# Order and placement around four TensorE waits in a hybrid conformer and stick-breaking decoder layer

## The chip, the cores and the metric

The kernel runs on one core of a Trainium2 chip. The metric is the device time of one execution in microseconds. The engines are TensorE (PE, with its weight loads shown as PEld), VectorE (DVE), ScalarE (ACT), GpSimd (POOL) and SyncE (SP); SP, ACT and POOL also issue DMAs, each in the order of its own queue. An engine executes its instructions in its program's order, so an instruction that waits holds up all that are queued behind it.

## What is computed

One decoder layer on x of 1024 tokens by 1024 channels, in float32:

```python
sh1, sc1, ga1, sh2, sc2, ga2 = split(silu(c) @ ada_w + ada_b, 6)
h = rmsnorm(x, pre_mix_g) * (1.0 + sc1) + sh1
# hybrid_mixer(h)
glu_in, qkv, gates = split(h @ w_in, ...)           # 1024, 1536 and 2048 columns
u = u_val * sigmoid(u_gate); u = causal_depthwise_conv(u, 31 taps)
y_conv = silu(layernorm(u)) @ w_conv_out
y_att = stick_breaking_attention(q, k, v) @ w_att_out   # 8 heads of 64
merged = sigmoid(g_conv) * y_conv + sigmoid(g_att) * y_att
x = x + ga1 * rmsnorm(merged @ w_o, post_mix_g)
h = rmsnorm(x, pre_ffn_g) * (1.0 + sc2) + sh2
y = (silu(h @ gate) * (h @ up)) @ w_ffn_out          # 2816 hidden channels
x = x + ga2 * rmsnorm(y, post_ffn_g)
```

## The kernel before, in words

Activations lie transposed: channels on the 128 partitions in tiles (index k or n, 8 of them), tokens along the free dimension in two halves of 512. Each float32 operand of a large product is split into a rounded high part (`hi`, a copy on ACT, called a cast here) and a low part (`lo`, the difference, on DVE). A product is then three matmuls, hi·hi, hi·lo and lo·hi, for each 128 rows of depth, so a product of depth 512 and 512 tokens is 12 matmuls. The gate and FFN products use a seven-product block scheme (the names s1 to s4, T1 to T4, B11 to B22, ka, kc): sums of weight blocks (s...) times sums of activation blocks (T..., B...).

Most instructions are put in order by a planner that simulates the engines; it takes what is ready, in the order of the program and of priorities. Some stretches are written out by hand and kept: `pin` ties each instruction of an engine to the one before it. Tiles come from pools; a tile of a tag takes the buffer of the one that had it `bufs` tiles earlier, and waits for that one's last reader. Pools are stacked in SBUF, so a pool that is opened after another was closed lies on the other's memory, and each of its tiles waits for the old tiles that it overlaps.

The stages that the change touches:

1. *Start (0 to 60 us).* PE, ACT and DVE are pinned. Per channel tile k, `shift_pe(k)` computes the shift column with 8 products of an `ada_w` tile (16 records in the trace, line 284), `shift_act(k)` (L288) moves it to `mod`, `x_op`, `hi_op` (L303) and `lo_op` (L306) make hhi[k] and hlo[k], and `gemm_q` (L321) adds the products of tile k to the first q, k and gate banks. Tiles 5 to 7 take their shift from DVE. In the loop over k, `shift_pe(kn + 2)` with kn = k + 1 stands ahead of the products of step k, so at k = 0 it is `shift_pe(3)`.
2. *Early gate products (about 400 to 462 us).* `early(i, q)` runs 14 times, in the order (0,0), (1,0), (0,1), (2,0), (1,1), (3,0), (2,1) and so on. One call casts half of a gate weight (`w_op`, hi on ACT L145, lo on DVE L413), runs a product into bank `k_i` (L426; q = 1 adds to the bank of q = 0), copies the bank to a tile `ee` (ACT, L665) and stores it from ACT's queue (L666). There are three banks, two buffers for `ee` (tag `sg`), three each for weights (`whi`, `wlo`) and raw weights. The planner orders it together with the making of the operands T1 to T4 (L701, L715 to L718).
3. *Hand-ordered FFN start (about 738 to 830 us).* The calls `ke` (early FFN products, L1146), `wh`/`wlo` (cast and low part of a weight, L145/L1079), `e` (copy and store of a result), `t12`, `t3`, `t4` (activation sums, L1165 to L1177), `hi_of`/`lo_of` (L1157/L1161), `b22h`/`b22l` (L1124/L1127) and the steps of two generators `r0 = ffn(0)`, `r1 = ffn(1)` are listed one after the other and pinned on PE, ACT and DVE. `next(r)` runs a generator to its next `yield`; the first step of `ffn(f)` for f > 0 makes the weight sums s1 and s2 on DVE (L1422, L1423) and the cast and low part of s2. Products are at L1037, the adds that take a product at L1439, L1454, L1457 and L1463.
4. *FFN's second product (from about 1160 us).* The pools of the FFN close (pv: eight `y2` tiles of 4 KB per partition, then nine `wt` tiles of 2 KB), and px and pg open in their place. `prep1` makes the operands of the first sweep: weights `wa` (cast L145, low part L1573) and gated activations `gb` (cast L145, low part L1567) in five buffers with the tag `gt`. `sweep` multiplies them at L1581. In px lie the output tiles of the first block (tag `xr`), in pg the operands and the small tiles `acc` and `rs` of the last norm.

Of the kernel before, what the change touches and what calls it, by code (L numbers as in the profile page):

```python
# [10 lines left out]
F32 = mybir.dt.float32  # L11
F32R = mybir.dt.float32r
AF = mybir.ActivationFunctionType
# [4 lines left out]
P = 128  # L18
D = 1024
T = 1024  # L20
KT = D // P
# [48 lines left out]
def tile_block(ctx: ExitStack, tc: tile.TileContext, xT, vecs, ada1, ada2, win, wv, wcv, wat, wo, w1, w2, cvw, out):  # L70
# [126 lines left out]
    with ExitStack() as s0:  # L197
# [119 lines left out]
        def gemm_q(b_, w, k, *sms, cs=(0, 1)):  # L317
            cols = slice(k * P, (k + 1) * P)
            for st, mv in sms:
                for c in cs:  # L320
                    pe.matmul(b_[c], w[st][:, cols], h[mv][k][:, hs[c]], start=(k == 0 and st == 0 and mv == 0),  # L321
                              stop=(k == KT - 1 and mv == 1))
# [31 lines left out]
        for k in range(KT):  # L354
            kn = k + 1
            if kn < KT:
                if kn not in SH_DVE:
                    shift_act(kn)
                if kn + 2 < KT and kn + 2 not in SH_DVE:
                    shift_pe(kn + 2)  # L360
                x_op(kn)
                if kn <= 2:
                    w0_hi(kn)
                hi_op(kn)
                if kn + 1 < KT:
                    dots(kn + 1)
                if kn <= 2:
                    w0_lo(kn)
            if k:
                lo_op(k)  # L370
            store(xm_d[k], xs[k])
            ws = list(zip((q0b, k0b, gg0b), w0s))
            if k == 0:
                gemm_q(*ws[0], 0, LH, HL)
                gemm_q(*ws[1], 0, HH, HL)
            elif k == 1:
                gemm_q(*ws[0], 1, HH, LH)
                gemm_q(*ws[1], 0, LH)
                gemm_q(*ws[1], 1, HH, LH)
                gemm_q(*ws[2], 0, HH, HL)  # L380
                gemm_q(*ws[2], 1, HH)
            else:
                for i, bw in enumerate(ws):
                    if k == 2 and i == 2:
                        gemm_q(*bw, 0, LH)
                        gemm_q(*bw, 1, LH)
                    gemm_q(*bw, k, HH, LH)
                    if k == KT - 1:
                        gemm_q(*bw, k - 1, HL)
                        gemm_q(*bw, k, HL)  # L390
                if k < KT - 1:
                    for bw in ws:
                        gemm_q(*bw, k - 1, HL)
# [16 lines left out]
    def w_op(name, src, hi_eng, lo_eng):  # L410
        t = wp.tile([P, 2, CH], F32R, tag=("whi", "wlo")[next(uid) % 2], name=name)
        copy_to(hi_eng, t[:, 0], src)
        lo_eng.tensor_tensor(t[:, 1], src, t[:, 0], op=ALU.subtract)  # L413
        return t[:, 0], t[:, 1]
# [14 lines left out]
    with ExitStack() as sC:  # L429
        pc = mkpool(sC, "pc")  # L430
        with ExitStack() as sA:
# [215 lines left out]
            for n in PLAIN:  # L647
                gb = banks2(f"pg{n}")
                gemm(gb, load_w(win[20 + n], f"wg{n}"), h, range(KT))
                for c in range(NCH):  # L650
                    sg = sgp.tile([P, CH], F32, tag="sg", name=f"sg{n}_{c}", bufs=2)
                    act.activation(sg, gb[c], AF.Sigmoid, bias=0.0, scale=1.0)
                    act.dma_start(s_d[n][:, c * CH:(c + 1) * CH], sg)
            kes = {}

            def early(i, q):
                if q == 0:
                    raw = wp.tile([P, T], F32, tag="wraw", name=f"ew{i}")
                    load(raw, win[20 + 2 * i])
                    kes[i] = bank(f"k_{i}"), raw  # L660
                k, raw = kes[i]
                w = w_op(f"a1{q + 1}_{i}", raw[:, q * CH:(q + 1) * CH], act, dve)
                prod0(k, w, ("B11", "B21")[q], q == 0)
                e = sgp.tile([P, CH], F32, tag="sg", name=f"ee{q}_{i}", bufs=2)
                act.activation(e, k, (AF.Copy, AF.Sigmoid)[q])  # L665
                act.dma_start(s_d[2 * i][:, :CH] if q else e_d0[i], e)  # L666

            for n, i in enumerate(GPAIRS):
# [258 lines left out]
    with ExitStack() as sF:  # L927
# [144 lines left out]
        def wh(key):  # L1072
            hi = wp.tile([P, T], F32R, tag="whi", name=f"w_{key}_hi")
            copy_to(act, hi, raws[key])
            wes[key] = hi
# [325 lines left out]
        def ffn(f):  # L1401
# [18 lines left out]
            if f:  # L1420
                s1, s2, s3 = wtmp(f"s1_{f}"), wtmp(f"s2_{f}"), wtmp(f"s3_{f}")
                dve.tensor_tensor(s1, a21, a22, op=ALU.add)  # L1422
                dve.tensor_tensor(s2, s1, a11, op=ALU.subtract)  # L1423
            s2o = w_op(f"s2o_{f}", s2, act, dve)
            yield
            s1o = w_op(f"s1o_{f}", s1, act, dve)
# [50 lines left out]
            yield  # L1477

        r0, r1 = ffn(0), ffn(1)
        for j in range(2):  # L1480
            t4(j)
        for j in (0, 1):
            hi_of("T1", j, h2[j, 0])
        ke(6, 1)
        wh(9)
        e(6, 1)
        for j in (2, 3):
            hi_of("T1", j, h2[j, 0])
        for j in range(2):
# [26 lines left out]
            b22h(j)  # L1516
        raw_w(1)
        next(r1)
        next(r0)
        next(r0)  # L1520
        for j in range(HK):
            b22l(j)
        next(r0)
        for j in (2, 3):
            t4(j)
        for j in (2, 3):
            lo_of("T4", j, h2[HK + j, 0])
        next(r1)
# [17 lines left out]
    with ExitStack() as sG:  # L1546
# [8 lines left out]
            return hp.tile([P, 2, CH], dt, tag="act", name=name)  # L1555

        def x_tile(name):
            return px.tile([P, 2, CH], F32, tag="xr", name=name, bufs=4)

        def bank(name):  # L1560
            return psg.tile([P, CH], F32, tag="main", name=name)
# [130 lines left out]
            return po_.tile([P, CH], F32, tag="wt", name=name, bufs=3)  # L1692

        def sum_sq(name, ys):
            acc = pg.tile([P, CH], F32, tag="acc", name=name, bufs=2)
            for n, y in enumerate(ys):
                if n == 0:
                    act.activation(acc, y, AF.Square)
                else:
                    sq = sq_tile(f"{name}_{n}")  # L1700
                    act.activation(sq, y, AF.Square)
                    add(dve, acc, acc, sq)
            return acc

        def finish(c, h, ps_sum, yy, last=None):
            n = ps_sum.shape[-1]
            cols = slice(h * n, (h + 1) * n)
            dcols = slice(c * CH + h * n, c * CH + (h + 1) * n)
            rs = pg.tile([P, CH], F32, tag="rs", name=f"frs{c}{h}", bufs=2)[:, :n]
            m, a = (sq_tile(f"frs{c}{h}{i}")[:, :n] for i in "ma")  # L1710
            rstd_from(rs, m, a, ps_sum, D)
            for m in range(4):
                y = ytile[yy[m // 2], m % 2]
                for i in range(2):
                    yi = y[:, i, cols]
                    if c == 0 and m < 2:
                        dve.tensor_tensor(yi, yi, rs, op=ALU.mult)
                    else:
                        src = last[2 * (m - 2) + i][:, cols] if last else yi
                        dve.scalar_tensor_tensor(yi, src, gpost2[:, 2 * m + i:2 * m + i + 1], rs, op0=ALU.mult,  # L1720
                                                 op1=ALU.mult)
                    if last:
                        add(dve, yi, yi, xq[2 * m + i])
                dst = out[2 * m:2 * m + 2, :, dcols].rearrange("n p t -> p n t")
                if last:
                    load(dst, y[:, :, cols])
                else:
                    acc = nc.gpsimd.dma_start(dst, y[:, :, cols], accum_op=ALU.add)
                    for i in range(2):
                        after_store(acc, c, 2 * m + i)  # L1730
# [142 lines left out]
```

## Time and profile before

| | us |
|---|---|
| median of 3 runs (1391.90 to 1392.66) | 1392.32 |
| the profiled execution | 1392.84 |
| its span, first to last instruction | 1391.1 |
| PE busy in it | 1364.4 |
| DVE busy | 1046.8 |
| ACT busy | 651.6 |
| POOL busy | 107.1 |
| granted clock of PE, mean | 0.997 |

In the profile's rows of the timeline the columns are: start in us from the span's start, duration in us, engine, line of the kernel, operation, tile written <- tiles read with buffer numbers left out, shapes, number of merged instructions (xcount), and in brackets how long the engine stood idle before it and what ended that. The letter q behind an engine marks its queue of DMA issues. Ends of matmuls are modelled, and consecutive ones overlap in the rows: a matmul of 512 columns is listed with 0.39 us while the next one starts 0.227 us after it. A wait is counted only where the engine had nothing left to run. In the rows of a tile, the three numbers before a stretch of time are the shortest, median and longest duration in ns.

### The profile page before, as it was taken

The page shows a single profiled execution, that of the slowest core. Times are in us where ns is not written, and L with a number is a line of the kernel's source. Part 1 is how long each engine was busy: PE and PEld are TensorE (multiplying, and loading weights), DVE is VectorE, ACT ScalarE, POOL GpSimd, SP SyncE. Part 2 cuts the span into 40 slices and gives each one's busy share as a digit, 9 for nine tenths or more (in the row PEclk, how much of TensorE's full clock was granted, in tenths as well). Part 3 has the DMA queues.
Part 4 walks back from the last instruction along what each step waited for, and adds up shares of the span by engine and source line. Part 5 has one row for each costly group of instructions (what it writes and reads, how often), then busy time and mean ns, then how long its engine had stood idle before and what let it go on. Part 6 is the DMA issues. An engine that isn't in the chain of part 4 may idle for free.

```text
span 1391.1 us, 18714 instructions
## 1 busy us (share of the span) xinstructions
PE 1364.4 (98%) x6778; PEld 1146.5 (82%) x6778; DVE 1046.8 (75%) x1600; ACT 651.6 (47%) x1147; POOL 107.1 (8%) x247
## 2 busy tenths in 40 slices
PE   7999999999999999999999999999999999999996
PEld 4898888998987888888887778888888887888886
DVE  7998686775858799777597987778877866784355
ACT  6475565464546457213365543324444444334441
POOL 0100000000000011000012100001111110000002
PEclk9999999999999999999999999999999999999998
DMA  9512051140468546955646545457776779586736
GB/s 384 216 35 80 16 167 46 46 136 32 136 199 304 201 131 239 334 184 194 265 137 195 198 139 179 144 189 253 241 244 245 263 255 389 167 343 218 247 108 122
DMA packets 94940, 265.01 MB, mean 191 GB/s; under 512 B 10048, under 2 KB 21440, under 8 KB 93824
## 3 DMA queue, kind: packets, MB, share of 16 engines
q1 hardware_dynamic: 74352, 201.68, 42.7%
q0 software_dynamic: 17904, 57.42, 11.8%
q10 hardware_dynamic: 2592, 4.72, 0.9%
q8 instruction: 53, 0.87, 0.3%
q14 instruction: 39, 0.32, 0.1%
HBM read 192.74 MB, written 71.04 MB: 190 GB/s over the span
## 4 chain that ended last, share of the span: by engine, by line
PE 93%; DMA 2%; ACT 2%; DVE 2%; issue 1%; SPq 0%; DVEq 0%; ACTq 0%
PE ka L1037 15%; PE ka L1581 9%; PE kc L1037 8%; PE pwo L955 6%; PE pb L1581 4%; PE ke L1146 4%; PE ka L426 4%; PE pgv L166 3%; PE pya L166 3%; PE pyc L777 3%; PE pv L503 3%; PE kc L426 2%; PE k L426 2%; PE pgg L166 2%; PE pk L166 2%; PE pcv L482 2%
## 5 line engine op out<-in xcount | busy, mean ns | idle before, releaser
L577 ACT ACTIVATE ka<-z 128x128 f32<-128x128 f32 (+2 forms) x96 | 47.3, 494 | 44.4 <-PE z L576 33.8
L1581 PE MATMUL ka<-gt,w2f 128*128 128x512 f32 x264 | 63.4, 389 | 0.0
L583 DVE TENSOR_TENSOR_SCAN ka<-ka,eye 128x128 f32<-128x128 f32 (+1 forms) x64 | 51.4, 815 | 11.9 <-ACT ka L577 11.8
L588 DVE TENSOR_TENSOR be<-be,ka 128x127 f32<-128x127 f32 (+2 forms) x96 | 53.8, 573 | 7.1 <-ACT be L579 2.0
L1581 PEld LDWEIGHTS ka<-gt,w2f 128*128 128x128 f32 x264 | 49.6, 188 | 10.3
L121 DVE SCALAR_TENSOR_TENSOR ada<-ada,cb 128x1024 f32<-128x1024 f32 x32 | 38.9, 1222 | 18.0 <-DMA ada<-in_ada_dram 17.8
L579 ACT ACTIVATE be<-z 128x127 f32<-128x127 f32 (+2 forms) x96 | 47.0, 496 | 5.6 <-PE tr L601 5.5
L601 PE MATMUL tr<-ident,be 128*128 128x128 f32 x288 | 46.5, 272 | 0.4 <-DVE be L588 0.4
L1146 PE MATMUL ke<-b,w_hi 128*128 128x512 f32 x176 | 44.5, 395 | 1.1 <-ACT w_hi L145 1.1
L586 DVE TENSOR_TENSOR_SCAN ka<-ka 128x512 f32<-128x512 f32 x32 | 40.6, 1275 | 3.7 <-ACT ka L577 3.6
L482 PE MATMUL pcv<-ph,cvw 128*128 128x128 f32 x320 | 42.9, 275 | 0.0
L607 ACT ACTIVATE ahi<-tr 128x512 fp32r<-128x512 f32 x48 | 28.3, 601 | 27.5 <-PE tr L601 19.4
L482 PEld LDWEIGHTS pcv<-ph,cvw 128*128 128x128 f32 x320 | 40.4, 191 | 0.7
L1146 PEld LDWEIGHTS ke<-b,w_hi 128*128 128x128 f32 x176 | 33.0, 188 | 9.2 <-ACT w_hi L145 1.5
L145 ACT ACTIVATE gt<-X 128x512 fp32r<-128x512 f32 x33 | 20.3, 629 | 39.0 <-DVE X L1624 13.1
L608 DVE TENSOR_TENSOR alo<-tr,ahi 128x512 fp32r<-128x512 f32 x48 | 32.1, 685 | 7.9 <-ACT ahi L607 7.6
L601 PEld LDWEIGHTS tr<-ident,be 128*128 128x128 f32 x288 | 34.8, 140 | 3.8 <-PE z L576 0.7
L145 ACT ACTIVATE s1o<-s 128x512 fp32r<-128x512 f32 x22 | 13.8, 629 | 50.4 <-PE ka L1037 43.5
L503 PE MATMUL pv<-wv_hi,hhi 128*128 128x256 f32 x128 | 36.8, 288 | 0.2 <-DVE klo L543 0.2
L426 PE MATMUL k<-hhi,a 128*128 128x512 f32 x112 | 35.4, 391 | 1.7 <-ACT ee L665 1.6
L503 PE MATMUL pv<-wv_hi,hlo 128*128 128x256 f32 x128 | 36.5, 285 | 0.0
L503 PE MATMUL pv<-wv_lo,hhi 128*128 128x256 f32 x128 | 36.2, 284 | 0.0
(551 smaller groups left out, 4154.9 us busy)
## 6 DMA issues: line engine op xcount, KB each, us to landing
w_d<-w2o POOLq DMA_DIRECT2D x44, 512.0 KB, 7.6
w2f<-w_d SPq DMA_DIRECT2D x44, 512.0 KB, 4.5
ada<-in_ada_dram SPq DMA_DIRECT2D x32, 512.0 KB, 5.5
w2r<-in_w_dram SPq DMA_DIRECT2D x44, 256.0 KB, 3.8
w1g<-in_w_dram SPq DMA_DIRECT2D x21, 512.0 KB, 3.7
w1u<-in_w_dram SPq DMA_DIRECT2D x21, 512.0 KB, 5.4
cvw<-in_cvw_dram SPq DMA_DIRECT2D x20, 512.0 KB, 3.7
ada_w<-in_ada_dram SPq DMA_DIRECT2D x8, 1024.0 KB, 13.8
```

What stands on the lines that cost most here:

```text
L166: pe.matmul(bank, st[:, cols], mv[k][:, c * CH:(c + 1) * CH], start=(i == 0 and s == 0), stop=(i == n - 1 and s == 2))
L426: pe.matmul(bank_, w[st][:, cols], mvs[mv], start=(first and j == 0 and s == 0), stop=(j == HK - 1 and s == 2), skip_group_check=not first)
L482: pe.matmul(cv[:, gi * TM:(gi + 1) * TM], wts[n][:, at:at + P], ph[:, g, SH - 1 - d:SH - 1 - d + TM], start=(d == 0), stop=(d == SH - 1))
L503: pe.matmul(pv[:, :256], st[k][:, tcols], mv[:, wc], start=(k == 0 and i == 0), stop=(k == KT - 1 and i == 2))
L577: act.activation(kap[:, s_lo:s_hi], z[:, zo:zo + w], AF.Sigmoid, bias=0.0, scale=-0.125)
L583: dve.tensor_tensor_scan(rev, rev, eye[:, CH - w:][:, ::-1], 0.0, op0=ALU.mult, op1=ALU.add)
L588: dve.tensor_tensor(beta[:, :m], beta[:, :m], kap[:, s_lo + 1:s_lo + 1 + m], op=ALU.mult)
L601: pe.transpose(tr[:, o:o + P], probs[ii][:, jo:jo + P], ident)
L955: pe.matmul(bank_, st[:, cols], mv[k][:, cs], start=(k == 0 and q == 0), stop=(k == KT - 1 and q == 2))
L1037: pe.matmul(bank_, st[:, cols], t[:, mv], start=(first and j == 0 and s == 0), stop=(j == HK - 1 and s == 2), skip_group_check=not first)
L1146: pe.matmul(kbs[f], wes[f][st][:, cols], t[:, mv], start=(i == 0 and j == 0 and st == 0 and mv == 0), stop=(j == HK - 1 and st == 1), skip ...
L1581: pe.matmul(dst, w[st][:, cols], g[mv], start=first and s == 0, stop=last and s == 2, skip_group_check=more)
```

## The change

Four edits in one:

1. `shift_pe(3)` moves from ahead of the products of k = 0 to behind them. The later ones keep their places.
2. From the fourth call of `early` on, the cast of a call on ACT is placed behind the result copy `ee` of the call three before. It is a tie of order on one engine, not a semaphore.
3. In the hand-written FFN start, `ke(6, 1)`, `wh(9)`, `e(6, 1)` go ahead of the first T4 and T1 operands; `ffn(1)` gets a `yield` between its sums s1, s2 and the cast of s2; the four `b22l` come directly behind those sums, ahead of the first two product steps of r0; the cast of s2 follows `t4(2)`, `t4(3)`.
4. `x_tile` has seven buffers and not four, `acc` and `rs` move from pg to px, and `rs` has three buffers and not two. px grows by 12 KB per partition for `xr` and by 10 KB for the other two, so the `gt` tiles of pg start that much further up.

```diff
@@ start
-                if kn + 2 < KT and kn + 2 not in SH_DVE:
+                if k and kn + 2 < KT and kn + 2 not in SH_DVE:
                     shift_pe(kn + 2)
...
                 gemm_q(*ws[1], 0, HH, HL)
+                shift_pe(3)
@@ early
-            kes = {}
+            kes, ees = {}, []
...
+                begin = len(nc.cur_bb.bb.instructions)
                 w = w_op(f"a1{q + 1}_{i}", raw[:, q * CH:(q + 1) * CH], act, dve)
+                if len(ees) > 2:
+                    for ins in nc.cur_bb.bb.instructions[begin:]:
+                        if ins.engine == mybir.EngineType.Activation:
+                            tc.add_manual_dep(ins, ees[-3], mybir.DependencyInfo(
+                                mybir.DependencyClass.NoSync, mybir.DependencyReason.SCHED_ONLY))
...
-                act.activation(e, k, (AF.Copy, AF.Sigmoid)[q])
+                ees.append(act.activation(e, k, (AF.Copy, AF.Sigmoid)[q]).ins.name)
@@ ffn
                 dve.tensor_tensor(s2, s1, a11, op=ALU.subtract)
+            if f == 1:
+                yield
             s2o = w_op(f"s2o_{f}", s2, act, dve)
...
         r0, r1 = ffn(0), ffn(1)
+        ke(6, 1)
+        wh(9)
+        e(6, 1)
         for j in range(2):
             t4(j)
         for j in (0, 1):
             hi_of("T1", j, h2[j, 0])
-        ke(6, 1)
-        wh(9)
-        e(6, 1)
...
         next(r1)
-        next(r0)
-        next(r0)
         for j in range(HK):
             b22l(j)
         next(r0)
+        next(r0)
+        next(r0)
         for j in (2, 3):
             t4(j)
+        next(r1)
         for j in (2, 3):
             lo_of("T4", j, h2[HK + j, 0])
@@ second product
-            return px.tile([P, 2, CH], F32, tag="xr", name=name, bufs=4)
+            return px.tile([P, 2, CH], F32, tag="xr", name=name, bufs=7)
...
-            acc = pg.tile([P, CH], F32, tag="acc", name=name, bufs=2)
+            acc = px.tile([P, CH], F32, tag="acc", name=name, bufs=2)
...
-            rs = pg.tile([P, CH], F32, tag="rs", name=f"frs{c}{h}", bufs=2)[:, :n]
+            rs = px.tile([P, CH], F32, tag="rs", name=f"frs{c}{h}", bufs=3)[:, :n]
```

## The prediction

> **What bounds the kernel now.** I read the page's engine list and its chain first, then the waits of TensorE (PE), then the order of time around each wait.
>
> ```profile
> span 1391.1 us, 18714 instructions
> PE 1364.4 (98%) x6778; PEld 1146.5 (82%) x6778; DVE 1046.8 (75%) x1600; ACT 651.6 (47%) x1147; POOL 107.1 (8%) x247
> ...
> PE 93%; DMA 2%; ACT 2%; DVE 2%; issue 1%; SPq 0%; DVEq 0%; ACTq 0%
> ```
>
> PE is busy 1364.4 of 1391.1 us and makes up 93% of the chain that ended last. The change takes no matmul away, so it can win only from the 26.7 us in which PE stands still, plus small stretches hidden inside "busy". The waits of PE over the whole span:
>
> ```profile
> PE psh L284 <- DMA ada_w<-in_ada_dram: 2.8, 2, 1.6
> ...
> PE k L426 <- ACT ee L665: 1.6, 1, 1.6
> PE ka L1581 <- ACT gb L145: 1.2, 1, 1.2
> PE ke L1146 <- ACT w_hi L145: 1.1, 1, 1.1
> PE ka L1037 <- DVE uw L1454: 0.5, 1, 0.5
> ```
>
> Columns: who waited, for whom, us in total, how often, the longest. These five rows hold 7.2 us, and each part of the change lies on one or two of them. Nothing later than these is tied to an absolute time: behind a mended wait, loads follow buffers that PE itself frees. So I count a gap closed on PE as time won at the end, unless the next operand is late there.
>
> One unit is used throughout, a product of 12 matmuls of 512 columns:
>
> ```profile
> 821.72 2.72 PE ka L1037 x12
> ```
>
> That is 2.72 us, 0.227 a matmul, when PE runs without gaps.
>
> **Part 1: the fourth shift product goes behind the k = 0 products.** It removes nothing; 16 matmul records (2.0 us) change place in PE's order, and no DMA and no other engine's instruction moves.
>
> ```profile
> 28.55 2.02 PE L284 MATMUL psh<-csb,ada_w 128*128 128x128 f32 x16 [1.58 <-DMA ada_w<-in_ada_dram]
> ...
> 32.26 1.95 PE L284 MATMUL psh<-csb,ada_w 128*128 128x128 f32 x16
> ...
> 58.99 0.62 PE L321 MATMUL pq<-hhi,w0hi 128*128 128x512 f32 x2
> ...
> 26.91 1.28 DVE L306 SCALAR_TENSOR_TENSOR hlo<-x,mod,hhi 128x1024 fp32r<-128x1024 f32 x1
> ...
> 57.13 2.59 DVE L306 SCALAR_TENSOR_TENSOR hlo<-x,mod,hhi 128x1024 fp32r<-128x1024 f32 x2
> ...
> 57.25 1.15 ACT L303 ACTIVATE hhi<-x,mod 128x1024 fp32r<-128x1024 f32 x1 [3.97 <-DVE x L300]
> ```
>
> PE now stands 1.58 us for the ada tile at 28.55, runs that product, then eight matmuls of k = 0 (1.8 us), then the next shift product at 32.26. After the change the eight come first. They need the low part of h, which VectorE (DVE) delivers at 26.91 + 1.28 = 28.19. So they run from 28.2 to 29.6 (the first two a little before), the shift product from 29.6 to 31.4, and PE is 1.0 us ahead at the second one. That lead is not kept whole. DVE has no idle time in this stretch and sets the rate: the high part for k = 7 is there at 57.25 + 1.15 = 58.40, where PE now arrives at about 59.1, and the last low part at 57.13 + 2.59 = 59.72. PE can gain 0.7 at the first and about 0.55 at the second, where what was the shift wait becomes a wait for hhi. Ends: 0 (DVE takes all of it) and 1.0. I take **-0.55**, nearest to the row of the last low part. The shift column of k = 3 is read two steps later on ScalarE (ACT), so its delay of 1 us is covered there; without that cover it would cost the same 1 us again.
>
> **Part 2: early gate casts after the result copy three calls back.** It adds order alone; ACT's 14 casts and 14 copies stay.
>
> ```profile
> 421.10 0.33 ACTq L653 DMA_DIRECT2D s_d<-sg  x1
> ...
> 425.18 0.58 ACT L665 ACTIVATE ee<-k 128x512 f32<-128x512 f32 x1
> 426.03 0.60 ACT L665 ACTIVATE ee<-k 128x512 f32<-128x512 f32 x1 [0.27 <-DMA s_d<-sg]
> ...
> 433.35 0.57 ACT L665 ACTIVATE ee<-k 128x512 f32<-128x512 f32 x1
> ...
> 418.61 0.39 PE L426 MATMUL k<-hhi,a 128*128 128x512 f32 x1
> ...
> 433.97 0.50 PE L426 MATMUL k<-hhi,a 128*128 128x512 f32 x1 [1.61 <-ACT ee L665]
> ```
>
> ```profile
> L145 ACT ACTIVATE a<-ew x14: 615/626/634, 397.9 to 443.4; 128x512 fp32r<-128x512 f32 x14
> L413 DVE TENSOR_TENSOR a<-ew,a x14: 680/684/693, 398.5 to 444.1; 128x512 fp32r<-128x512 f32 x14
> ...
> DMA to landing us min/median/max: 2.0/4.1/6.7
> ```
>
> (The last row is of the copies' stores: from issue to landing.) PE's sixth early product waits 1.61 us for the third copy, which stood on ACT behind casts for later products. With the tie those casts come behind it. But two things speak against booking 1.61. First, a copy also needs one of two buffers, freed when a store lands: the second copy visibly waited for a landing, and the first copy's store, issued no earlier than 425.8, may land as late as 432.5, so the third copy may hardly come earlier than that. Second, today the third product that PE runs, at 418.61 + 2 x 2.72 = 424.05, is the one of call 3 (its bank is free and its cast was made long before; the casts begin at 397.9). Its cast is now tied behind the first copy, which came at 425.18. PE then has only call 2 left, which adds to the bank that this copy reads: a new wait from 424.05 to 425.2 or 425.75, 1.1 to 1.7 us. Afterwards the loop is copy 0.6 + cast 0.63 + low part 0.68 + product 2.72 = 4.6 us against three products, 8.2 us, so 3.5 us are left for a late landing. Behind each tied cast on ACT stand later casts and copies, and on SP the loads of the next gate weights move by up to 7 us, since their buffers are freed by the casts; by my estimate the first weight pair of the next stage then still lands some 3 us before its product. Ends: -1.6 (wait gone, none new) and +1.7 (new one, old one kept). I take **-0.2**: one wait given for another.
>
> The row gives 4.1 us for a store of 256 KB. [...]
>
> **Part 3: the hand-ordered FFN start.** No instruction is added; the order on ACT and DVE (pinned here) changes, PE's order does not. SP's and POOL's DMAs only follow their buffers, earlier.
>
> ```profile
> 784.04 0.64 ACT L1157 ACTIVATE T_0o<-y 128x512 fp32r<-128x512 f32 x1 [1.47 <-DVE y L1177]
> ...
> 786.28 1.04 ACT L145 ACTIVATE w_hi<-w_raw 128x1024 fp32r<-128x1024 f32 x1
> ...
> 787.37 2.11 PE L1146 MATMUL ke<-b,w_hi 128*128 128x512 f32 x8 [1.07 <-ACT w_hi L145]
> ...
> 787.35 1.22 DVE L1079 TENSOR_TENSOR w_lo<-w_raw,w_hi 128x1024 fp32r<-128x1024 f32 x1 [1.29 <-ACT w_hi L145]
> ```
>
> Moving ke(6,1), wh(9), e(6,1) ahead puts the cast of weight 9 before the four T4/T1 casts. Its buffer is weight 6's, last read by ke(6,1), the last product but one before the wait (786.14 - 5.44 = 780.7 to 783.4, where 786.14 is the wait's start less the modelled tail of 0.16); ACT idled 1.47 us until 784.04, so the cast fits at 782.6 to 783.6 and the T casts hardly move. The low part then ends near 787.2; PE, starting at 786.14, wants it eight matmuls in, at 787.95. The wait goes: -1.07, next late is nothing.
>
> ```profile
> 801.11 0.84 PE L1037 MATMUL ka<-T_0o,s2o 128*128 128x512 f32 x3
> ...
> 814.31 1.24 PE L1037 MATMUL ka<-T_2o,a 128*128 128x512 f32 x3
> ...
> 816.09 0.85 PE L1037 MATMUL ka<-T_0o,s2o 128*128 128x512 f32 x3
> ...
> 804.96 0.69 DVE L1028 TENSOR_TENSOR s2o<-s,s2o 128x512 fp32r<-128x512 f32 x1 [2.59 <-ACT s2o L145]
> ...
> 810.75 0.75 DVE L1127 SCALAR_TENSOR_TENSOR B_3o<-y,mod,B_3o 128x512 fp32r<-128x512 f32 x1
> ...
> 812.01 0.69 DVE L1454 TENSOR_TENSOR uw<-ka,uw 128x512 f32<-128x512 f32 x1
> ...
> 814.72 0.69 DVE L1161 TENSOR_TENSOR T_3o<-y,T_3o 128x512 fp32r<-128x512 f32 x1
> ```
>
> The five products of f = 0 run from 801.11 to 816.09, 14.98 us against 5 x 2.72 = 13.60: 1.38 lost at the end, on B22's low parts, on uw and on T4's low parts. The cause is DVE: it idles 2.59 us for the cast of f = 1's s2, then does everything late. In the new order the four B22 low parts (2.65 us) fill that hole. With PE 1.07 ahead, T3 ends at 808.2 and uw's add runs at 808.4 to 809.1, now bound by PE; then two T4 operands on DVE (1.4), two casts and the s2 cast of f = 1 on ACT (0.6 each), the s2 low part, and T4's low parts end at 812.95 and 813.55. B22 runs to 810.92 without a wait, and T4's third operand is wanted at 812.5: 0.45 still lost. Gain 1.38 - 0.45 = 0.93. If the s2 low part is slower to come, T4's lows wait behind it and the gain falls to 0.3; the ends of the part are -1.07 and -2.45. I take **-2.0**. f = 1's own products want s2's low part at 814.1, 1.8 us after it is there.
>
> **Part 4: where the gated operands' tiles lie.** No operation moves in the program; the pool px grows by three x tiles and takes acc and rs, so the tiles "gt" of pg start higher: over the FFN's short-lived weight temporaries instead of over its y2 tiles, which hold p1, uw and the w2 forms until their stores land.
>
> ```profile
> 1161.76 0.63 ACT L145 ACTIVATE wa<-wa 128x512 fp32r<-128x512 f32 x1 [1.36 <-PE ka L1037]
> 1162.29 2.70 ACT L145 ACTIVATE gb<-X 128x512 fp32r<-128x512 f32 x5
> ...
> 1162.96 1.20 PE L1581 MATMUL ka<-gb,wa 128*128 128x512 f32 x4 [1.24 <-ACT gb L145]
> ...
> 1148.77 0.68 DVE L1028 TENSOR_TENSOR s4o<-s,s4o 128x512 fp32r<-128x512 f32 x1
> ```
>
> All five first gb casts stand behind a weight cast that waits for the FFN's last product. The temporaries' last read is at 1148.77, so the planner can put the casts before 1161 on an ACT that idles between its jobs. Then PE starts at once: 1.24, plus about 0.3 inside the first four matmuls (1.20 against 0.91), where the low part is late. The next limit may be the bank that the FFN's last add on DVE still reads then. Ends: 0 (order unchanged) and -1.5; I take **-1.3**, near the wait's row. rs with three buffers and acc's place change nothing: PE runs into the tail without waiting for them.
>
> **Sum.** -0.55 - 0.2 - 2.0 - 1.3 = -4.05. The profiled execution took 1392.84 (span 1391.1 and 1.74 around it), 0.52 above the median 1392.32. Against its own time the sum is 1388.8; against the median **1388.3**.
>
> **Rivals.** (a) *Absorbed or reordered*: the planner makes the unpinned orders anew from parts 2 and 4, and PE, which lost almost nothing there, meets a new wait of about the size of those in the table (1 to 1.6), or part 4's casts stay behind the weight cast. Then only parts 1 and 3 minus one wait remain: 1392.3 - 2.55 + 1.2 = 1391.0, within 0.2%. For it: the table holds only four waits behind part 1, so a new order has little to win. Against: the orders in parts 1 and 3 are written out, not planned. (b) *Buffers, not order*: the early stage's wait lies on two store buffers, so the tie only moves it; part 2 gives +1.5 (new wait kept, old one nearly kept) while the rest holds: 1390.0, the same side as (a). [...]
>
> ```profile
> 461.41 0.60 ACT L665 ACTIVATE ee<-k 128x512 f32<-128x512 f32 x1 [2.00 <-PE k L426]
> ```
>
> (c) *Slower*: each tied cast waits for a copy that waits for a landing. Two buffers serve two products, 5.44 us; less copy and issue, 0.7, a store may take 4.7 us. The median is 4.1, the worst 6.7. If stores took 6.2 under this load, each of the 11 tied calls would cost (6.9 - 5.44)/2 = 0.73 us, 8.0 in all: 1388.5 + 8.0 = 1396.5. It decides from 4.7 us on; today's copies, the last of which is the row above, keep a pace of (461.4 - 425.2)/13 = 2.78, so just about not.
>
> **How the numbers follow.** 0.2% is 2.8 us, about what a measurement of this kernel can tell from no change: faster means under 1389.5, slower over 1395.1. The forecast (3 to 5.7 us won) gets 0.58; (a) 0.20 and (b) 0.15, both mostly within 0.2%; (c) 0.07. A sixth of (b) ends below 1389.5, so faster 0.60, same 0.33, slower 0.07. The range runs from all upper gains of the parts that are sure of their sign, 1392.3 - 0.7 - 0.7 - 2.45 - 1.5 = 1386.9, with half a microsecond under it, to the far end of (a), one more wait than there: 1392.0. The forecast's own range is 1386.6 to 1389.4.
>
> **What would show it.** Part 1: no ada_w wait before the k = 0 products, and a wait for hhi or hlo of about 0.3 before k = 7. Part 2: the wait on ee gone from the sixth product, and one of 1.1 to 1.7 before the third. Part 3: no wait of ke on w_hi; B22 without a gap; 0.3 to 0.6 inside the T4 product of f = 0. Part 4: gb casts before 1160 and no PE wait for them. The prediction is wrong if PE shows a new wait between 60 and 400 us or after 1165, if DVE, not PE, carries the first 60 us further than k = 7, or if the early products fall to the landing pace.

## The result and the profile after

| | before | after |
|---|---|---|
| median of 19 runs each, on the same chips | 1392.84 us | 1390.37 us |
| ratio, with its 95% interval | | 0.9983 (0.9976 to 0.9991) |
| a profiled execution | 1392.84 | 1390.05 |
| its span | 1391.1 | 1388.3 |
| PE busy in it | 1364.4 | 1364.1 |

The change wins 2.5 us, 0.17% (0.09 to 0.24): clear of the noise and inside the stated range, which ends at 1392.0, but outside the forecast's own range of 1386.6 to 1389.4, and under the 0.2% that the prediction took as its bound for "faster". It is three fifths of the 4.05 us forecast. (The 1392.32 of the table before is the median of the first three runs; all comparisons below are with runs of before in the same series.) The ratios leave out two executions far beyond the others of their kernel, one of before at 1521.66 us and one of the kernel with later ties at 7898.52.

After, the page's span and chain, and the waits of PE over the span:

```profile
span 1388.3 us, 18714 instructions
...
PE 93%; DVE 2%; DMA 2%; ACT 1%; issue 1%; SPq 0%; DVEq 0%; ACTq 0%
```

```profile
PE k L427 <- ACT ee L672: 1.4, 1, 1.4
PE psh L284 <- DMA ada_w<-in_ada_dram: 1.3, 1, 1.3
PE ka L1591 <- ACT gb L145: 1.2, 1, 1.2
PE psh L284 <- ACT mod L288: 0.7, 2, 0.3
PE pq L321 <- DVE hlo L306: 0.5, 1, 0.5
...
PE psx L988 <- DVE xsum L1121: 0.4, 1, 0.4
PE ka L1044 <- DVE T_2o L1168: 0.3, 1, 0.3
```

Line numbers grew by up to ten: L427 is the early gate product (L426 before), L672 the result copy, L1044 the FFN product, L1591 the sweep. Against the waits of before: one of the two ada waits is gone, but a wait of 0.5 for `hlo` is new and the wait of `psh` for `mod`, 0.4 once before, now comes twice; the wait of `ke` for the weight part is gone; in the FFN start the wait of 0.5 for `uw` is gone, and one of 0.3 for an operand T_2o is left; the wait of the early products is 1.4 in place of 1.6; the sweep's wait for gb is still there, at 1.2; a wait of `psx` for `xsum`, 0.4, is new.

Where the time went is best read as a waterfall. I took the start of the first matmul of each stage from the timeline rows of both kernels; the table gives the change of each stage's length, changed kernel less before, and the same for each part alone (the runs come below). Each column is one execution.

| stretch, with its times before (us) | after | part 1 | part 2 | part 3 | part 4 |
|---|---|---|---|---|---|
| to the first q product, 0 to 22.9 | +0.27 | -0.56 | -0.42 | -0.54 | -0.59 |
| first layer products, to 73.1 | -0.13 | -0.11 | -0.03 | -0.02 | 0.00 |
| attention, to 418.6 | +0.07 | -0.46 | +0.18 | +0.08 | +0.12 |
| early gate products and gates, to 602.0 | -1.21 | +0.52 | +1.20 | +0.50 | +0.08 |
| out-projection, to 734.6 | +0.38 | +0.01 | +0.68 | +0.01 | +0.02 |
| hand-ordered FFN start, to 944.0 | -2.14 | +0.02 | +0.02 | -2.15 | -0.06 |
| FFN, to the sweep at 1163.0 | 0.00 | +0.66 | 0.00 | 0.00 | 0.00 |
| sweeps, to the last matmul at 1379.2 | 0.00 | 0.00 | -0.01 | -0.01 | 0.00 |

The first row hangs on when the first loads land: ACT's last `sq` starts behind the last load of x, at 14.71 us before and at 14.96 in the changed kernel, 0.25 of the 0.27. In the other rows the columns of parts 3 and 4 show what a stage with an unchanged order may differ between two executions: at most 0.12, but 0.5 in the gate stage. Part 1's -0.46 and +0.66 also lie in stages whose order it leaves alone; they are scatter that I can't name. Part 2's +0.68 in the out-projection goes almost wholly between 651.9 and 653.4 us; with part 1 or part 2 alone the planner orders that stage anew, and with both it is back, by tile names, at the order of before.

### The profile page after: what moved, and what is told of

It is laid out like the page before. It is cut to its first block, busy times and chain, and to the rows that moved or that the text cites. A ratio compares the mean times of both kernels' runs of the same rounds, so it can differ in the third digit from the quotient of the medians.

```text
span 1388.3 us, 18714 instructions
## 1 busy us (share of the span) xinstructions
PE 1364.1 (98%) x6778; PEld 1147.2 (83%) x6778; DVE 1046.9 (75%) x1600; ACT 651.7 (47%) x1147; POOL 107.4 (8%) x247
## 4 chain that ended last, share of the span: by engine, by line
PE 93%; DVE 2%; DMA 2%; ACT 1%; issue 1%; SPq 0%; DVEq 0%; ACTq 0%
PE ka L1044 15%; PE ka L1591 9%; PE kc L1044 8%; PE pwo L962 6%; PE ke L1153 4%; PE pb L1591 4%; PE ka L427 4%; PE pgv L166 3%; PE pyc L784 3%; PE pya L166 3%; PE kc L427 3%; PE pv L504 3%; PE pgg L166 2%; PE pk L166 2%; PE k L427 2%; PE pcv L483 2%
## 5 line engine op out<-in xcount | busy, mean ns | idle before, releaser
L1591 PE MATMUL ka<-gt,w2f 128*128 128x512 f32 x264 | 63.4, 389 | 0.0
L1591 PEld LDWEIGHTS ka<-gt,w2f 128*128 128x128 f32 x264 | 49.5, 188 | 10.3
L427 PE MATMUL k<-hhi,a 128*128 128x512 f32 x112 | 34.9, 390 | 1.4 <-ACT ee L672 1.4
```

The costliest lines, as they stand in the source:

```text
L427: pe.matmul(bank_, w[st][:, cols], mvs[mv], start=(first and j == 0 and s == 0), stop=(j == HK - 1 and s == 2), skip_group_check=not first)
L1591: pe.matmul(dst, w[st][:, cols], g[mv], start=first and s == 0, stop=last and s == 2, skip_group_check=more)
```

## The experiments

My theory when I began: part 3 did what was forecast, part 2 also cleared other gaps of the gate stage, part 1's gain was taken by the next thing in line, and part 4 did nothing because ACT's planned order, not the tiles, holds the gated casts. The rivals were the sizes of the prediction.

**Each part alone, on the kernel before.** One line of each edit, of those shown in the change:

```diff
part 1: +                if k and kn + 2 < KT and kn + 2 not in SH_DVE:
part 2: +                if len(ees) > 2:
part 3: +        ke(6, 1)
part 4: +            return px.tile([P, 2, CH], F32, tag="xr", name=name, bufs=7)
```

> Only the later shift products, on the kernel before. My present theory, read from the two traces: the wait of 1.58 us that the edit removes comes back in pieces (a wait for the low part of the first weight, one for the low part of the first activations, one for the shift column 2), so the end of the first stage stands about 0.13 us earlier than before, and the whole kernel 0.1 to 0.2 us earlier (1392.6 to 1392.8 where the kernel before has 1392.84). The planner's new order also moves the third-stage psx wait: if the shift alone brings that order, 0.3 to 0.4 us are lost there near 715 us, and the whole is 0.1 to 0.3 us later instead. Rival, the prediction's size: 0.55 us earlier, 1392.3.

> Only the tie of the early casts to the result copies, on the kernel before. Theory from the traces: the gate stage as a whole gives about 1.2 us (from 418 to 602 us), with a new wait of about 1.4 us before the third product and none before the sixth; if the later psx wait near 715 us comes along, 0.4 us of it is given back, so the whole is 0.8 to 1.2 us earlier (1391.6 to 1392.0). Rival, the prediction's size: 0.2 us earlier, 1392.6, with the rest of the gate stage unchanged.

> Only the FFN's hand-written order, on the kernel before. Theory: the wait for the weight part before the out-projection's last products (1.07 us) and most of the wait at the fourth product of block 0 (0.93 us) go, nothing else moves: 2.0 to 2.1 us earlier, 1390.7 to 1390.9, with a residual wait of 0.3 us inside that fourth product. Rival: the FFN loop behind it absorbs part, then under 1.5 us (above 1391.3).

> Only the moved tile pools, on the kernel before. The order of instructions on every engine is the one of before; only addresses and the semaphores of the gated operands' casts change. Theory: the scalar engine's order holds those casts behind the sixth weight cast, so the wait of about 1.25 us before the sweep's first product stays and the time is that of before, 1392.8 within 0.3. Rival, the prediction: the casts run before 1160 us and the wait goes, 1.3 us earlier, 1391.5.

Measured, against 1393.11 for before: part 1 1393.27 (ratio 1.0001, 0.9992 to 1.0010), part 2 1392.68 (1.0000, 0.9991 to 1.0008), part 3 1390.87 (0.9986, 0.9977 to 0.9995), part 4 1393.22 (1.0007, 0.9998 to 1.0016). Part 3 alone is 2.2 of the 2.5 us won. Part 1's whole time shows no gain; its own stage is 0.11 shorter in the profile, the present theory's size and not the 0.55 of the prediction. The order of no engine differs between part 4 and before, and its waiting cast stands where it stood:

```profile
1161.33 0.63 ACT L145 ACTIVATE wa<-wa 128x512 fp32r<-128x512 f32 x1 [1.36 <-PE ka L1037]
1161.86 0.61 ACT L145 ACTIVATE gb<-X 128x512 fp32r<-128x512 f32 x1
```

Part 2's time is the 1392.6 of the rival, but not for the rival's reason, and the profile contradicts both expectations: the gate stage was 1.20 *longer*, though its order there is, by tile names, that of the changed kernel, whose stage was 1.21 shorter. The cause shows in its third product and in the windows around it (the columns: length, PE busy with its number of matmuls, PEclk, the share of DMA, GB/s), part 2 alone first, the changed kernel second:

```profile
425.96 0.50 PE L426 MATMUL k<-hhi,a 128*128 128x512 f32 x1 [2.03 <-ACT ee L671]
...
424.00:426.00 2.00, 0.04 (x1) 1.00 1.02 418
426.00:430.00 4.00, 4.00 (x11) 0.58 0.85 271
```

```profile
424.00:426.00 2.00, 0.62 (x3) 1.00 1.02 410
426.00:430.00 4.00, 4.00 (x18) 1.00 0.88 292
```

PE stood 2.03 us for the first copy and then ran 11 matmuls in four microseconds where the changed kernel ran 18; the granted clock was 0.58. Seven matmuls fewer, at 0.227 us each, are 1.6 us: about eight intervals of 427 ns in place of 227. This execution (1394.46) is one of four of the eleven, 1393.29 to 1394.52, whose mean granted clock is 0.995 or 0.996; the other seven, at 0.997 or 0.998, took 1391.90 to 1392.91. I come back to it below.

**Part 4's cause: order or place.** On the changed kernel, one tie of order on ACT, in `prep1`:

```diff
             gs = [op2(f"gb{q}1_{j}", x[:, q - 1], act, dve) for q in (1, 2)]
...
+            gcast.extend(i.name for i in nc.cur_bb.bb.instructions[begin:] if i.engine == mybir.EngineType.Activation)
...
+            ws.append(wop2(f"wa12_{j}", w[:, 1], act, dve))
+            if j == 2:
+                for i in nc.cur_bb.bb.instructions[begin:]:
+                    if i.engine == mybir.EngineType.Activation:
+                        tc.add_manual_dep(i, gcast[2], mybir.DependencyInfo(
+                            mybir.DependencyClass.NoSync, mybir.DependencyReason.SCHED_ONLY))
...
```

> The changed kernel with one move on the scalar engine: the sixth weight cast of the first sweep, the one that waits for the FFN's last product, stands behind the first five gated casts. Theory (the order holds those casts, not their tiles): they run before 1159 us, the sweep's first product starts at 1158.8 to 1159.0 in place of 1160.2, its wait of 1.24 us shrinks to 0.1 to 0.3 (the fourth matmul still needs the vector engine's last FFN product), and the kernel is 1.0 to 1.3 us earlier than the changed one: 1389.1 to 1389.4 against 1390.4, 0.997 to 0.998 of before. Rival (tiles, or the loads of the gated operands): the casts do not start before 1159.5, the wait stays, 1390.4.

Measured: 1389.97 against 1393.16 (0.9972, 0.9963 to 0.9980). The timeline of ACT, then of PE:

```profile
1158.31 0.63 ACT L1468 ACTIVATE uw<-uw 128x512 f32<-128x512 f32 x1
1158.85 2.70 ACT L145 ACTIVATE gb<-X 128x512 fp32r<-128x512 f32 x5
1161.45 0.62 ACT L145 ACTIVATE wa<-wa 128x512 fp32r<-128x512 f32 x1
```

```profile
1159.43 0.84 PE L1044 MATMUL ka<-T_3o,a 128*128 128x512 f32 x3
1160.11 1.45 PE L1591 MATMUL ka<-gb,wa 128*128 128x512 f32 x4
```

The casts begin 1.26 us before PE wants them, and the sweep starts 0.68 us after the first matmul of the last FFN group, with no wait. (This execution runs 1.3 us late from the gate stage on, so its casts stand at 1158.85 and not before.) The FFN stretch is 1.40 shorter, of which 0.30 is given back in the sweeps, nearly all of it inside the first four matmuls (1.45 against 1.19): 1.1 net. So on the moved tiles it was ACT's order that held the casts; whether the place matters too, the kernel without part 4 shows below.

**Part 1's cause: the PSUM tile.** The shift sums lie in one tile of PSUM, the memory that this kernel's products are written to.

```diff
-        psh = ps0.tile([P, 4, P], F32, name="psh")
+        psh = [ps0.tile([P, 2, P], F32, name=f"psh{i}") for i in range(2)]
...
-                pe.matmul(psh[:, k % 4], ...
+                pe.matmul(psh[k % 2][:, k // 2 % 2], ...
```

> The changed kernel with the shift sums in two PSUM tiles, even and odd slots, in place of one; the order on every engine is unchanged. Theory A (the tile couples slots): the scalar engine's shift column 2 no longer waits for the products of shift 3 (1.09 us of idle time there), the shift products of 4 no longer wait 0.35 us for it, and the first stage ends 0.3 to 0.4 us earlier. Theory B: the vector engine's row, unbroken in these microseconds, sets the pace of the first stage, and the same 0.3 to 0.4 us stand as a wait at the next low part: 0 within 0.1. In both the whole time moves by less than this measurement can tell.

Measured: 1390.02 against 1393.16 (0.9976, 0.9967 to 0.9984), as the changed kernel within the interval; the stage of the first layer products is 0.04 shorter than before's, not shorter than the changed kernel's. The rows of shift product 4 in the changed kernel and in this one:

```profile
32.28 2.05 PE L284 MATMUL psh<-csb,ada_w 128*128 128x128 f32 x16 [0.35 <-ACT mod L288]
...
31.97 0.26 ACT L288 ACTIVATE mod<-psh,vec 128x1 f32<-128x1 f32 x1 [1.09 <-PE psh L284]
```

```profile
31.57 2.02 PE L284 MATMUL psh<-csb,ada_w 128*128 128x128 f32 x16 [0.24 <-DMA ada_w<-in_ada_dram]
```

ACT's 1.09 us of idling for the neighbour slot is gone, so the one tile did couple the slots (A's mechanism; whether the tile counts or the piece of PSUM under it, two tiles do not tell). The size is B's, but for neither's reason: the product now waits 0.24 us for its ada tile, which lands just then. The loads were dense there, 419 and 425 GB/s in the two stretches of the changed kernel; that they make the tile late was not tried:

```profile
20.00:28.00 8.00, 6.32 (x46) 5.09 (x44) 7.72 (x12) 4.07 (x7) 0.72 (x1) 1.00 1.03 425
28.00:36.00 8.00, 7.18 (x47) 6.38 (x47) 7.93 (x12) 3.89 (x6) 1.10 (x2) 1.00 1.01 419
36.00:44.00 8.00, 8.00 (x37) 6.62 (x36) 7.93 (x11) 2.45 (x3) 1.07 (x2) 1.00 1.01 416
```

The last row also says that PE (first number after the length) has no gap from 36 to 44 us, although DVE (third) is full too; the next wait in PE's rows is at 70.94 us.

**Part 2's new wait: two ways to take it away.** Either the ties begin one call later, so that the third product is again one with a bank of its own, or the first two results get buffers of their own.

```diff
-                if len(ees) > 2:
+                if len(ees) > 3:
```

> The changed kernel with the ties beginning one early cast later, so that the third product is again the first half of pair 2, which uses a bank of its own, and not the second half of pair 0, whose bank the first copy must leave. Theory (the new wait at the third product is for that bank, and the bank is held by the copy that waits for the store of the earlier gate tiles): no wait of over 0.3 us at the third product, none comes in its place at the fourth to sixth, the gate stage is 1.2 to 1.5 us shorter than the changed kernel's, 1389.0 us. Rival (the ring of two result tiles sets the rate of the products): the wait moves to the fifth or sixth product with 1.3 to 1.8 us, and the time is 1390.4.

```diff
-                e = sgp.tile([P, CH], F32, tag="sg", name=f"ee{q}_{i}", bufs=2)
+                e = (pa.tile([P, CH], F32, tag="beta", name=f"ee{q}_{i}", bufs=4) if len(ees) < 2 else
+                     sgp.tile([P, CH], F32, tag="sg", name=f"ee{q}_{i}", bufs=2))
```

> The changed kernel, all ties kept, with the first two early results in tiles of their own (idle attention tiles) in place of the ring of two that they share with the gate tiles. The planner then also puts several residual casts later. Theory (first copy held by the store of the gate tiles): the first copy runs at 421.5 to 422.5 us in place of 425.2, the third product, still the second half of pair 0, starts without a wait, and the gate stage is 1.2 to 1.5 us shorter than the changed kernel's, 1389.0 us, unless the moved residual casts make a wait of their own behind 450 us. Rival (the order of the scalar engine holds the copy): the copy stays behind 425 us and the wait of 1.4 us stays.

The later ties: 1389.02 against 1393.16 (0.9967, 0.9956 to 0.9978). No wait for a copy is left among its waits; the ones that remain are old:

```profile
PE ka L1591 <- ACT gb L145: 1.2, 1, 1.2
...
PE psx L988 <- DVE xsum L1121: 0.4, 1, 0.4
PE ka L1044 <- DVE T_2o L1168: 0.3, 1, 0.3
```

The gate stage is 2.02 shorter than before's, 0.8 more than the changed kernel's; I had expected 1.2 to 1.5, and the rest is lost in four small gaps at the sixth product (0.64 in all). The own buffers: 1407.33 (1.0101, 1.0084 to 1.0117), a clear miss in time, and no proof of the mechanism either. ACT's first copy, then PE's waits:

```profile
420.51 0.60 ACT L673 ACTIVATE ee<-k 128x512 f32<-128x512 f32 x1 [1.92 <-PE k L427]
...
434.82 0.63 ACT L145 ACTIVATE T2o<-f 128x512 fp32r<-128x512 f32 x1 [1.26 <-DVE f L725]
```

```profile
PE lnm L800 <- DVE la L798: 5.3, 1, 5.3
PE ka L427 <- ACT s2o L145: 4.3, 1, 4.3
```

The copy ran at 420.51, as soon as its product was done, where the changed kernel has it at 425.18, and the third product did not wait. But the planner also put the casts of the next stage's operands behind the copies (the first T2 at 434.8, at 418.0 in the changed kernel), so buffer and order changed together. The changed kernel's own rows speak for the order: its first copy stands right behind four such casts and waits for nothing else.

```profile
424.66 0.61 ACT L145 ACTIVATE T4o<-f 128x512 fp32r<-128x512 f32 x1
425.18 0.57 ACT L672 ACTIVATE ee<-k 128x512 f32<-128x512 f32 x1
```

In other executions of the same order the store of the gate tiles comes later than these casts and adds 0.18 to 0.44 us. So both hold the copy, to within half a microsecond of each other, and the rival was not refuted. With its own buffers the kernel then stood 5.3 us for a sum on DVE and 4.3 us for a weight cast; how the new order led there was not followed up.

**Both mends together, and with part 1 or part 4 undone.**

> The changed kernel with both mends: ties one early cast later, and the sixth weight cast of the first sweep behind the first gated casts. Theory: the two add, the gate stage is 0.8 us shorter than the changed kernel's by the profile and has no pause of over 0.5 us, so no stretch of low granted clock behind one; the sweep's first product follows the FFN within 0.3 us, net 1.1 us: 1.9 us under the changed kernel, 1388.4 median, 0.9965 of before. Rival: the planner re-sorts something else when both are there, and one of the two is lost: 1389.0 to 1389.5.

> The kernel with both mends, but with the shift products where they were before (part 1 undone). The planner then leaves the order of the out-projection's products and of two vector sums near 715 us as it was with the ties alone. Theory (part 1 brought the wait before psx through the planner): the wait of 0.55 and 0.4 us there is gone, the first stage is 0.1 us longer, and the whole is 0.5 to 0.9 us earlier than with part 1. Rival: the wait before psx is bound by the vector engine's sums in any order, and stays: 0.1 us later than with part 1.

> The kernel with both mends, but with the tile pools where they were before (part 4 undone); the order on every engine is that of the kernel with both mends. Theory (place and order both bind, in series): with the order mended the gated casts now wait for the tiles under them, to the vector engine's last FFN product at 1159.7 us in the changed kernel's time, and the sweep's first product waits 1.0 to 1.3 us again: 1.0 to 1.3 us later than with part 4. Rival (the place never mattered): the casts run as early, and the time is that of the kernel with both mends within 0.2 us.

Measured against 1393.05: both 1388.18 (0.9966, 0.9953 to 0.9978); without part 1 1387.70 (0.9961, 0.9948 to 0.9973); without part 4 1387.83 (0.9963, 0.9949 to 0.9976). The two mends add as expected, and all three are ahead of both kernels; among them the times decide nothing. The rows do. Without part 4 the casts start as early, 1.26 us ahead of the sweep as with it, and the sweep starts without a wait, on the tiles of before:

```profile
1155.06 0.63 ACT L1468 ACTIVATE uw<-uw 128x512 f32<-128x512 f32 x1
1155.60 2.70 ACT L145 ACTIVATE gb<-X 128x512 fp32r<-128x512 f32 x5
...
1156.86 1.44 PE L1591 MATMUL ka<-gb,wa 128*128 128x512 f32 x4
```

The order of every engine is the same in both, so the place does not matter for this wait. Without part 1 my expectation failed: the wait before `psx` is there still,

```profile
PE psx L987 <- DVE xsum L1120: 0.4, 1, 0.4
```

so part 1 did not bring it. (That profile, of the longest of its five executions, also shows a wait of 0.74 us for an operand `mhi` at 650 us; its out-projection is 1.69 longer than before's.) What did bring the wait before `psx` stays open: it is in the changed kernel and in all that I built on it but the one with own buffers, and in no part alone. The rows show where it sits. DVE's adds to `xsum`, before and in the changed kernel:

```profile
713.62 2.28 DVE L1114 TENSOR_TENSOR xsum<-xsum,xr 128x512 f32<-128x512 f32 x3
```

```profile
712.62 1.48 DVE L1121 TENSOR_TENSOR xsum<-xsum,xr 128x512 f32<-128x512 f32 x2
714.58 0.69 DVE L1121 TENSOR_TENSOR xsum<-xsum,xr 128x512 f32<-128x512 f32 x1 [0.47 <-ACT w_o_hi L145]
```

Before, three adds run on end; now the third stands 0.47 us until ACT has cast a weight that it does not read, though by tile names ACT and DVE have the order of before there.

**The varying pause.** The eleven times of the kernel with the moved weight cast fall into two groups, five from 1388.68 to 1389.08 and six from 1389.97 to 1391.11; the profiled execution, 1390.33, was of the second. One more execution of the same kernel:

> The kernel with the moved weight cast once more, unchanged, to see another of its executions. Theory (the length of the pause before the third early product varies with the landing of the gate tiles' store, and a pause from about 1.8 us on is followed by some 3.4 us of half granted clock): if the pause is 1.75 us or less, the matmuls behind it keep 227 ns and the execution takes 1388.7 to 1389.1 us; if it is 1.83 or more, eight intervals of 427 ns follow and it takes 1389.9 to 1390.4. Rival (the half clock has nothing to do with the pause): a pause and a dip occur in other combinations, or the two groups of times show the same intervals.

It took 1388.74. Its third product and the windows behind it, after those of the first execution:

```profile
425.18 0.50 PE L427 MATMUL k<-hhi,a 128*128 128x512 f32 x1 [1.83 <-ACT ee L672]
...
426.00:430.00 4.00, 4.00 (x12) 0.57 0.86 256
```

```profile
425.68 0.50 PE L427 MATMUL k<-hhi,a 128*128 128x512 f32 x1 [1.67 <-ACT ee L672]
...
426.00:430.00 4.00, 4.00 (x19) 1.00 0.82 263
```

A pause 0.16 us shorter, and the clock stays whole: as the theory has it, and against the rival. The mean clocks of the eleven fit it but for one: 0.997 in all five of the first group, 0.995 or 0.996 in five of the second, but 0.998 in the sixth (1390.26). No edit set the length of the pause; it fell as it did.

## Why the prediction was right or wrong

The total fell inside the wide range in part by luck. Against the sum of -4.05, part 4 gave 1.3 too little, part 1 0.42 too little and part 2 about 1.0 too much, while 0.38 was lost at a place that the prediction had not named. The measured 1390.37 lies nearer to the rivals' 1391.0 and 1390.0 than to 1388.3.

**Part 3** (-2.0): right in mechanism and size, -2.14 in the changed kernel and -2.15 alone. The wait of `ke` for the weight part left, B22 ran without a gap, and the residue inside the fourth product is 0.32 where 0.45 was worked out:

```profile
812.06 0.73 PE L1044 MATMUL ka<-T_2o,a 128*128 128x512 f32 x2 [0.32 <-DVE T_2o L1168]
```

**Part 1** (-0.55): mis-sized; 0.13, and 0.11 alone. The failed step is "PE is 1.0 us ahead at the second one" (its own times give 32.26 - 31.4 = 0.86). It moved the shift product of k = 3 but did not ask for the next: counted from the first q product, that one starts at 9.08 us (32.28 - 23.20) where before had 9.33 (32.26 - 22.93), so 0.25 ahead. It waits 0.35 for the column that shares its PSUM tile, and with that mended, 0.24 for its own ada tile. The second failed step is "DVE has no idle time in this stretch and sets the rate": DVE was full, but PE's rows show no wait from there to 70.94 us either, so there was no wait for hhi to be found.

**Part 2** (-0.2): both waits came out as written, the one at the sixth product gone and a new one of 1.38 before the third, inside the 1.1 to 1.7 forecast. The sum was mis-sized in two directions. It counted these two waits only; the new order also closed a wait of `ka` for `s2o`, 0.4 in the profile of before and 0.8 in those of parts 1 and 3, and some small gaps, so the stage won 1.21. And it had no term for what a longer pause does to the clock: with a pause of 2.03 us, and a clock of 0.58 behind it, the same order made the stage 1.20 longer. The rival "buffers, not order" tells a part of the new wait: in the changed kernel the copy that ends it stood behind casts on ACT, as shown, and in the execution of part 2 alone it waits 0.44 more for the store of the gate tiles:

```profile
425.31 0.60 ACT L671 ACTIVATE ee<-k 128x512 f32<-128x512 f32 x1 [0.44 <-DMA s_d<-sg]
```

**Part 4** (-1.3): wrong, 0. The failed step is "so the planner can put the casts before 1161": that tiles are free earlier does not make the planner order anything earlier, and it did not. The end "0 (order unchanged)" and the second half of rival (a) name what happened. The sign "gb casts before 1160" came true without the mechanism: they start at 1159.53 only because everything ahead of them was 2.76 us earlier. The size was near, once the order was mended: 1.40 came out of that wait, 0.30 of it was lost again in the sweeps, where the prediction had counted on a further gain of about 0.3.

**Not foreseen:** 0.38 given back before `psx`, open as said. The stages in the column of the changed kernel add to -2.76 us; its span, given to the tenth, is 2.8 shorter. The changed kernel also shows a wait of 0.16 at 74.68, in the stretch where a new wait was to prove the prediction wrong; of the two profiled executions of the kernel with the moved weight cast, one has it and the other does not, so it is scatter.

## What to carry to other kernels

A wait on a cast can have two holders, the buffer and the queue (here the queue held the sweep's casts, for which PE stood 1.24 us, and the early copy had both, to within 0.44 us); look at what stands directly ahead of the waiting instruction on its engine before moving memory, and test by moving one instruction. When a stall is closed, work out the landing of the *next* load and the state of the *next* bank before booking the gain (here 0.24 us for the next ada tile, and 1.38 us for the next bank). And where a pause cannot be removed, its length counts: here the low clock behind a pause of 1.83 us cost 1.6 us more.

## What the hardware showed

After some pauses of PE in full work the granted clock dropped for a while. Behind single pauses of 1.38 (changed kernel), 1.61 (before), 1.67 (the moved weight cast, second execution) and 1.74 us (two PSUM tiles) the clock read 1.00 in the four microseconds from 426 on (in before from 434 on), with 18 or 19 matmuls of 512 columns in them. Behind pauses of 1.83 (the moved weight cast, first execution) and 2.03 us (part 2 alone) it read 0.57 and 0.58 from 426 on, with 12 and 11 matmuls: seven fewer, which costs 1.6 us. The first execution of the moved weight cast took 1390.33 us and the second 1388.74, 1.59 apart. The low rate does not begin with the restart. The next rows still start 0.23 to 0.24 us a matmul apart; the first pair that takes clearly longer than the usual 0.63 us (1.06 and 0.99) begins 1.27 and 0.58 us behind the restart.

The length of one pause is not the whole of it. In the kernel with own buffers PE stood twice for 0.8 us, with 0.7 us of work between, and the clock fell too (the wait, then the windows around the second pause and behind it):

```profile
PE k L427 <- ACT a L145: 1.6, 2, 0.8
...
444.00:446.00 2.00, 1.21 (x4) 0.85 1.02 412
446.00:449.00 3.00, 3.00 (x8) 0.53 1.05 405
```

Behind the pauses of 5.3 and 4.3 us of that kernel the clock read 0.50 and 0.57:

```profile
464.00:468.00 4.00, 4.00 (x9) 0.50 0.35 137
...
551.00:555.00 4.00, 3.66 (x9) 0.57 0.39 150
```

So one pause of 1.83 us, or two of 0.8, came before a fall, and one of 1.74 did not bring it. Whether the edge for one pause lies fixed between 1.74 and 1.83 us or moves, or whether the idle time in some stretch counts, was not tried.
